# Stick-breaking attention on one core: two sliver tiles joined into one of 64 columns, and a few steps of the heads put at other units

## The chip, the cores and the metric

The kernel runs on one core of a Trainium2 chip. The metric is the device time of one execution in microseconds; the time before is 2059.08 us, the median of 3 runs (2058.46 to 2063.94). Engines are named as in the profile: PE (matmuls), PEld (its weight loads), DVE (vector), ACT (scalar), POOL (GpSimd) and SP (it issues the DMAs here).

## The reference, cut to what matters

One inference step of a decoder layer: a combined input projection, eight heads of stick-breaking attention and four of gated linear attention, a gate per branch, an output projection and two norms. There are 1024 prompt tokens behind 16 learned meta tokens (1040 rows) and 8 x 4 sampled tokens with paged caches. The change concerns the prompt's attention:

```python
def stick_break_weights(z, mask):
    sp = jnp.where(mask, jax.nn.softplus(z), 0.0)
    later = lax.cumsum(sp, axis=z.ndim - 1, reverse=True) - sp
    return jnp.where(mask, jnp.exp(jax.nn.log_sigmoid(z) - later), 0.0)

def sb_attend(qb, qpos, k, v, kpos, bias):
    a = stick_break_weights(sb_logits(qb, k, bias), kpos[None, :] < qpos[:, None])
    return jnp.einsum('bhqk,bkhd->bqhd', a.astype(v.dtype), v)
```

The mask is strict: a key counts only for later queries. The weight of a key is reduced by the softplus of all later keys that the query sees, so the work on one query goes from the last key to the first and hands a sum on (the carry).

## The kernel before, in words

Products of full float32 precision are made of three matmuls on a high part (rounded to float32r) and a low part (the rest): high by high, high by low, low by high. ACT makes a high part by a copy that rounds, DVE the low part by a subtraction.

**Heads.** `head(h)` runs the input projections of V, K and Q for one head, each by `inproj`: 16 blocks of rows for three chunks of tokens, in 24 groups of six matmuls into three PSUM accumulators (L342 to L344). After each group `W.beat()` moves a small scheduler, the Weaver, by one unit: whatever generator is due emits its next instructions there, up to its next `yield n`, which puts it off by n units. A head is 72 units. The attention of head h is woven in this way into the projections of head h+1. The order on each engine is then the program's order as the framework's scheduler sets it out; each engine works in its order, and waits on semaphores. A manual dependency without a semaphore (`spread`, `behind`) only sets that order: `spread` puts an instruction behind `W.mark`, the newest matmul of a projection.

**Tiles of attention.** Keys lie in nine tiles of 126 (`KT`) in the columns 1 to 126 of 128; column 0 holds the carry and column 127 nothing. Queries lie in two blocks, qi = 0 (positions 16 to 527) and qi = 1 (528 to 1039). `attend` spawns a tile per key tile and query block, from the last key tile to the first: (1,8) to (1,0), then (0,4) to (0,0). A tile has as many columns as queries that see some key of it. (1,8) has 32 and (0,4) has 24: these are the slivers. All others have 150 to 512.

`attend_tile` is one tile's generator:
- the scores z: three matmuls (L589 to L591) into a PSUM tile; X = softplus of z by DVE (L595, L598) and ACT (L596, L597); POOL's mask where the tile crosses the diagonal (L601);
- two units later, and when the predecessor's carry is there: the carry's copy into row 0 of X (L607), and the split of X, `hi_s` on ACT and `lo_s` on DVE (L574, L575 in `split_tmp`, which all splits share);
- D1 = 4 units later the correction: two matmuls with a triangle of -1 (L610, L611), which add to z; then Y = exp(z) on ACT (L615), its mask on POOL (L617), and in the same unit the split of Y, `hi_a` and `lo_a`;
- D2 = 6 units later the values: three matmuls (L623 to L625) into the query block's accumulator `O`; behind the block's last tile ACT copies it out (L628) and SP stores it (L629).

Unit by unit after the end of a head's Q projection, the scores, split of X, correction and values stand at 2, 4, 8, 14 for (1,8); at 40, 42, 46, 52 for (0,4); at 49, 54, 58, 64 for (0,1); at 53, 58, 62, 68 for (0,0).

**Keys and values of a head.** `ev_k` copies a chunk of projected keys to a staging tile and spawns `split_k`, which fills the two key tiles `kt` (high and low, one buffer each, so they come free with the last score matmul of the previous head, that of (0,0)): eight pieces in all, an ACT copy (L693) and a DVE subtraction (L694) for each, all pieces of a chunk in one unit. `load_v` runs in the three units behind the Q projection: a POOL memset of a staging tile (L561), the loads of V rows by 126 (L562, L564), the high part on ACT (L566), the low part on DVE (L568).

Around this, DVE works through the dot products of the sampled queries with the paged keys (L464), and SP issues the pages' loads. Staging tiles come from one pool of seven.

Of the kernel before, what the change touches and what calls it, by code (L numbers as in the profile page):

```python
# [10 lines left out]
F32 = mybir.dt.float32  # L11
# [5 lines left out]
ALU = mybir.AluOpType  # L17
# [3 lines left out]
P = 128  # L21
# [6 lines left out]
NSMP = NB * NT  # L28
T = META + SEQ + NSMP
REAL = META + SEQ  # L30
# [10 lines left out]
KT = 126  # L41
# [43 lines left out]
def hybrid_step(ctx: ExitStack, tc: tile.TileContext, x_prompt, x_sample, cache_k, cache_v, state_gla,  # L85
# [3 lines left out]
    nc = tc.nc  # L89
    mm = nc.tensor.matmul  # L90
    vec, act, pool = nc.vector, nc.scalar, nc.gpsimd
# [17 lines left out]
    W = Weaver()  # L109

    def stage(nm, dt=F32):
        return stg.tile([P, 384], dt, tag="stg", name=nm)
# [39 lines left out]
    znd = dram.tile([NSMP, HEADS, NSMP], F32, name="znd")  # L152
# [37 lines left out]
    with tc.tile_pool(name="xp", bufs=2) as xp, tc.tile_pool(name="xps", bufs=5, space=PSUM) as xps:  # L190
# [336 lines left out]
    with tc.tile_pool(name="sp", bufs=1) as sp, tc.tile_pool(name="sps", bufs=1, space=PSUM) as sps:  # L527
# [26 lines left out]
        def load_v(h, V, behind):  # L554

            for c in range(3):
                st = stage(f"vr{h}_{c}")
                sv = st[:].rearrange("p (a d) -> p a d", d=P)
                nt = 3 if c < 2 else 2
                src = new_v_prompt[0, 0, :, h, :]  # L560
                pool.memset(st[:], 0.0)  # L561
                nc.sync.dma_start(sv[1:KT + 1, :nt], src[c * 378:c * 378 + nt * KT].rearrange("(a p) d -> p a d", p=KT))  # L562
                if c == 2:
                    nc.sync.dma_start(sv[1:33, 2, :], src[8 * KT:REAL])  # L564
                vs = slice(3 * c, 3 * c + 3)
                ins = act.copy(V[0][:, vs, :], sv)  # L566
# [8 lines left out]
            vec.tensor_tensor(b[:rows, :n], X, a[:rows, :n].bitcast(F32), ALU.subtract)  # L575
            return a, b

        def attend_tile(h, qi, qlo, qhi, j, jmax, q, kt, V, carry, O):
            nm = f"{h}_{qi}_{j}"
            k0 = j * KT  # L580
            nk = P
            c0 = max(qlo, k0)
            col = c0 - qlo
            n = qhi - c0
            qs = slice(c0 - META, c0 - META + n)
            ks = slice(j * P, j * P + nk)
            z = sps.tile([P, 512], F32, tag="z", bufs=4, name=f"z{nm}")
            zz = z[:nk, :n]
            mm(zz, kt[0][:, ks], q[0][:, qs], start=True, stop=False)  # L589
            mm(zz, kt[0][:, ks], q[1][:, qs], start=False, stop=False)  # L590
            mm(zz, kt[1][:, ks], q[0][:, qs], start=False, stop=True)  # L591
# [3 lines left out]
            vec.tensor_scalar(X, zz, bias, 30.0, ALU.add, ALU.min)  # L595
# [4 lines left out]
            if w > 0:  # L600
                pool.affine_select(X[:, :w], X[:, :w], [[1, w]], ALU.is_gt, 0.0, base=c0 - k0 + 1, channel_multiplier=-1)  # L601
            yield 2
            if j < jmax:
# [6 lines left out]
            mm(zz, ntri0[:nk, :nk], sh[:nk, :n], start=False, stop=False, skip_group_check=True)  # L610
            mm(zz, ntri0[:nk, :nk], sl[:nk, :n], start=False, stop=True, skip_group_check=True)  # L611
# [4 lines left out]
            if w > 0:  # L616
                pool.affine_select(Y[:, :w], Y[:, :w], [[1, w]], ALU.is_gt, 0.0, base=c0 - k0 + 1, channel_multiplier=-1)  # L617
# [7 lines left out]
            mm(o[:, col:], V[1][:nk, j, :], ah[:nk, :n], start=False, stop=(j == 0), skip_group_check=True)  # L625
            if j == 0:
                st = sp.tile([P, 512], F32, tag="X", bufs=3, name=f"ost{h}_{qi}")
                act.copy(st[:], o[:])  # L628
                nc.sync.dma_start(od[h][:, qlo - META:qhi - META], st[:])  # L629

        def attend(h, q, kt, V):

            carry, O = {}, {}
            for qi, j in ORDER:
                qlo, qhi = ((16, 528), (528, REAL))[qi]
                n = qhi - max(qlo, j * KT)
                W.spawn(attend_tile(h, qi, qlo, qhi, j, (qhi - 1) // KT, q, kt, V, carry, O))
# [10 lines left out]
        def sample_q(h, qsm, ks):  # L648

            ps = sps.tile([P, 512], F32, tag="z", bufs=4, name=f"qst{h}")  # L650
            nc.tensor.transpose(ps[:NSMP, 0:P], qsm[:], ident[:])
            qtok = stage(f"qtok{h}")[:NSMP, :P]
            act.copy(qtok, ps[:NSMP, 0:P])
            nc.sync.dma_start(qsd[:, h * P:(h + 1) * P], qtok)
            ps = sps.tile([P, 512], F32, tag="z", bufs=4, name=f"zn{h}")
            mm(ps[:NSMP, :NSMP], ks[:], qsm[:], start=True, stop=True)
            zns = sp.tile([NSMP, NSMP], F32, tag="zns", name=f"zns{h}")
            act.copy(zns[:], ps[:NSMP, :NSMP])
            nc.sync.dma_start(znd[:, h, :], zns[:])
            yield 4  # L660
            heads_ready.append(h)

        def head(h):
# [15 lines left out]
            kt = [sp.tile([P, KW], F32R, tag=f"k{i}", name=f"k{i}_{h}") for i in range(2)]  # L679
# [3 lines left out]
            ks = sp.tile([P, NSMP], F32, tag="ks", name=f"ks{h}")  # L683

            def split_k(raw, c, lo, hi):
                at, end = lo, min(hi, REAL)
                while at < end:
                    j, off = divmod(at, KT)
                    n = max(1, (end - at) // KT) if off == 0 else 1
                    w = min(KT - off, end - at)  # L690
                    d = [t[:, j * P:(j + n) * P].rearrange("p (a x) -> p a x", a=n)[:, :, off + 1:off + 1 + w] for t in kt]
                    r = raw[:, at - lo:at - lo + n * w].rearrange("p (a x) -> p a x", a=n)
                    act.copy(d[0], r)  # L693
                    vec.tensor_tensor(d[1], r, d[0].bitcast(F32), ALU.subtract)  # L694
# [3 lines left out]
                return  # L698
                yield
# [21 lines left out]
            V = values(h, copied[-1])  # L721
# [15 lines left out]
    with tc.tile_pool(name="gp", bufs=1) as gp, tc.tile_pool(name="gps", bufs=1, space=PSUM) as gps:  # L737
# [323 lines left out]
        for g in range(GH):  # L1061
            kt = gp.tile([P, T], F32, tag="k", name=f"gk{g}")
# [227 lines left out]
    with ExitStack() as out:  # L1290
# [349 lines left out]
        kept = []  # L1640
# [53 lines left out]
```

## Time and profile before

| | |
|---|---|
| time, median of 3 runs | 2059.08 us |
| the profiled execution | 2062.69 us |
| its span | 2061.0 us |
| granted TensorE clock | 0.998 |
| head phase with attention | 116 to 960 us of the span, about |

The span reaches from the first to the last instruction of the program that the profile holds; the execution's time is a little longer. Busy time is the union of an engine's instructions. A matmul's start is exact, while its end is modelled, and matmuls that follow each other overlap; what one of them costs is read from the distance of starts. "Idle before" a group is the time that its engine had nothing to do just ahead of it, with what ended it.

### The profile page before, as it was taken

To read this page: it belongs to the slowest core of one execution; us is meant where nothing else is said; L and a number is where in the kernel's file an instruction comes from. 1 tells how busy PE (TensorE), PEld (TensorE's weight loads), DVE (VectorE), ACT (ScalarE), POOL (GpSimd) and SP (SyncE) were. 2 spreads that over 40 slices of the span, in tenths; PEclk is the share of its full clock that TensorE was granted. 3 is DMA by queue.
4 is the path that set the end of the run, shared out by engine and by line. 5 is a ranking of instruction groups with operands and counts; after the bars stand their busy time and mean duration, and the time that the engine had idled before them with its cause. 6 is when DMAs were issued, how large, how long until landed. Compare 5 with 4: busy or idle time off the path is not lost.

```text
span 2061.0 us, 41982 instructions
## 1 busy us (share of the span) xinstructions
PE 2023.1 (98%) x12507; PEld 1864.4 (90%) x12507; DVE 1551.5 (75%) x6282; ACT 953.5 (46%) x2293; POOL 85.1 (4%) x304
## 2 busy tenths in 40 slices
PE   6999999999999999999999999999999999999998
PEld 5999999999999998999999999999888898788776
DVE  7368989888988989899898888978444347554566
ACT  7355555565655556433534335343433325432332
POOL 0012000101000000000000000000000000000000
PEclk9999999999999999999999999999999999999999
DMA  6344454645455452443433434335776666352475
GB/s 202 104 139 147 140 158 134 169 134 147 146 157 147 141 126 73 138 107 80 108 103 80 126 81 115 93 87 166 241 228 230 222 227 195 134 163 75 148 272 175
DMA packets 371821, 301.85 MB, mean 146 GB/s; under 512 B 42360, under 2 KB 312104, under 8 KB 371592
## 3 DMA queue, kind: packets, MB, share of 16 engines
q1 hardware_dynamic: 371288, 298.64, 48.5%
q8 instruction: 98, 1.61, 0.3%
q14 instruction: 131, 1.07, 0.2%
q10 hardware_dynamic: 304, 0.53, 0.1%
HBM read 241.75 MB, written 57.31 MB: 145 GB/s over the span
## 4 chain that ended last, share of the span: by engine, by line
PE 84%; DVE 7%; DMA 3%; ACT 3%; issue 2%; SPq 1%; POOL 0%; DVEq 0%; ACTq 0%; POOLq 0%
PE acc_g L342 5%; PE acc_g L343 5%; PE acc_g L344 5%; PE b L1595 4%; PE b L1597 4%; PE b L1596 4%; PE acc_gv L342 3%; PE acc_gv L343 3%; PE acc_gv L344 3%; PE acc_k L342 3%; PE acc_k L344 3%; PE acc_k L343 3%; PE acc_v L342 2%; PE acc_v L344 2%; PE acc_v L343 2%; PE acc_q L342 2%
## 5 line engine op out<-in xcount | busy, mean ns | idle before, releaser
L464 DVE SCALAR_TENSOR_TENSOR jk<-kp,qb 128x128 f32<-128x128 f32 x2048 | 592.9, 289 | 43.2 <-DMA qb<-qsd 1.5
L342 PE MATMUL acc_g<-hT,wh_g 128*128 128x368 f32 (+2 forms) x768 | 251.1, 327 | 0.5 <-DVE ga L389 0.5
L343 PE MATMUL acc_g<-hT,wh_g 128*128 128x368 f32 (+2 forms) x768 | 247.2, 322 | 0.0
L344 PE MATMUL acc_g<-hT,wl_g 128*128 128x368 f32 (+2 forms) x768 | 246.8, 321 | 0.0
L1595 PE MATMUL b<-ring,f 128*128 128x512 f32 x416 | 164.7, 396 | 4.7 <-DVE u L1465 2.1
L464 DVE DVE_READ_ACCUMULATOR jk<-kp,qb 128x1 f32 x2048 | 166.7, 81 | 0.0
L1596 PE MATMUL b<-ring,f 128*128 128x512 f32 x416 | 163.3, 392 | 0.2 <-DVE ring L1395 0.2
L1597 PE MATMUL b<-ring,f 128*128 128x512 f32 x416 | 162.5, 391 | 0.0
L342 PEld LDWEIGHTS acc_g<-hT,wh_g 128*128 128x128 f32 x768 | 144.3, 188 | 13.1 <-issue 11.2
L1395 DVE TENSOR_TENSOR ring<-wr,ring 128x512 fp32r<-128x512 f32 x104 | 71.3, 689 | 102.4 <-ACT ring L1394 100.2
L343 PEld LDWEIGHTS acc_g<-hT,wh_g 128*128 128x128 f32 x768 | 144.4, 188 | 0.7
L344 PEld LDWEIGHTS acc_g<-hT,wl_g 128*128 128x128 f32 x768 | 144.2, 188 | 0.0
L1394 ACT CAST ring<-wr 128x512 fp32r<-128x512 f32 x104 | 64.2, 620 | 143.4 <-PE b L1597 83.7
L342 PE MATMUL acc_gv<-hT,wh_gv 128*128 128x400 f32 (+2 forms) x384 | 130.3, 339 | 0.0
L342 PE MATMUL acc_k<-hT,wh_k 128*128 128x384 f32 (+1 forms) x384 | 126.3, 329 | 0.0
L343 PE MATMUL acc_gv<-hT,wh_gv 128*128 128x400 f32 (+2 forms) x384 | 125.2, 326 | 0.0
L342 PE MATMUL acc_q<-hT,wh_q 128*128 128x368 f32 (+2 forms) x384 | 124.9, 325 | 0.0
L344 PE MATMUL acc_gv<-hT,wl_gv 128*128 128x400 f32 (+2 forms) x384 | 124.6, 325 | 0.0
L344 PE MATMUL acc_k<-hT,wl_k 128*128 128x384 f32 (+1 forms) x384 | 124.6, 324 | 0.0
L343 PE MATMUL acc_k<-hT,wh_k 128*128 128x384 f32 (+1 forms) x384 | 124.4, 324 | 0.0
L344 PE MATMUL acc_q<-hT,wl_q 128*128 128x368 f32 (+2 forms) x384 | 123.3, 321 | 0.0
L343 PE MATMUL acc_q<-hT,wh_q 128*128 128x368 f32 (+2 forms) x384 | 123.2, 321 | 0.0
(454 smaller groups left out, 5288.7 us busy)
## 6 DMA issues: line engine op xcount, KB each, us to landing
kp<-in_cache_k_dram SPq DMA_DIRECT2D x512, 64.0 KB
vr<-in_cache_v_dram SPq DMA_DIRECT2D x64, 512.0 KB
tf<-in_w_out_dram SPq DMA_DIRECT2D x64, 256.0 KB
td<-tf SPq DMA_DIRECT2D x64, 256.0 KB
qb<-qsd SPq DMA_DIRECT2D x64, 256.0 KB
wr_g<-in_w_in_dram SPq DMA_DIRECT2D x64, 256.0 KB
wr<-td SPq DMA_DIRECT2D x56, 256.0 KB
wr<-in_w_out_dram SPq DMA_DIRECT2D x48, 256.0 KB
```

The costliest lines, as they stand in the source:

```text
L342: mm(acc[c][:, :n], wh, hh[k][:, lo:hi], start=(k == 0), stop=False)
L343: mm(acc[c][:, :n], wh, hl[k][:, lo:hi], start=False, stop=False)
L344: W.mark = mm(acc[c][:, :n], wl, hh[k][:, lo:hi], start=False, stop=(k == NK - 1)).ins
L464: ins = vec.scalar_tensor_tensor(jk[:], kp[:], 1.0, qbs[h, b][:, t, :], ALU.mult, ALU.mult, accum_out=zt[:, t, NPG - 1 - i:NPG - i])
L1394: act.copy(wh, r)
L1395: vec.tensor_tensor(wl, r, wh.bitcast(F32), ALU.subtract)
L1595: mm(bk[:], ah, wh, start=first and k == 0, stop=False, skip_group_check=True)
L1596: mm(bk[:], ah, wl, start=False, stop=False, skip_group_check=True)
L1597: mm(bk[:], al, wh, start=False, stop=last and k == 7, skip_group_check=True)
```

## The change

- (1,8) and (0,4) run as one tile, j = 8, of 64 columns, first in the head: columns 0 to 31 are the last 32 queries of block 0, columns 32 to 63 the last 32 of block 1. Key tile 8 gets the 24 keys of (0,4) in its columns 32 to 55 (two POOL copies out of key tile 4), and V's rows for them come by one more load. Two POOL steps mask it (`causal`). The carry of block 0 is kept in a small SBUF tile, that of block 1 stays in PSUM. Its values go to an accumulator of their own, are copied to a small tile, and are added by DVE to the last 32 columns of each block's output behind the copy L628.
- (0,4) is no longer spawned, so (0,3) comes at unit 40. By the same counting the units of (0,1) are 47, 50, 54, 60 and those of (0,0) are 51, 54, 58, 64.
- In every tile the split of Y comes one unit behind Y (`yield 1`, then `D2 - 1`): the values stay where they were.
- `split_k` yields behind each piece, and chunk c begins 3c units later.
- The memsets of V's staging tiles are put behind `W.mark` by `spread`.
- The scores among sampled tokens (`zns`) take a staging tile in place of a tile of their own.

```diff
                 src = new_v_prompt[0, 0, :, h, :]
-                pool.memset(st[:], 0.0)
+                spread(pool.memset(st[:], 0.0))
...
                 if c == 2:
-                    nc.sync.dma_start(sv[1:33, 2, :], src[8 * KT:REAL])
+                    nc.sync.dma_start(sv[1:32, 2, :], src[8 * KT:REAL - 1])
+                    nc.sync.dma_start(sv[32:56, 2, :], src[4 * KT:4 * KT + 24])
...
+            both = j == 8
-            n = qhi - c0
+            n = 64 if both else qhi - c0
...
+            def queries(t):
+                if both:
+                    return t[:].rearrange("p (a x) -> p a x", a=2)[:, :, 480:512]
+                return t[:, qs]
+
+            def causal(t):
+                if both:
+                    t = t.rearrange("p (a x) -> p a x", a=2)
+                    pool.affine_select(t, t, [[1 - 24, 2], [1, 32]], ALU.is_gt, 0.0, base=24, channel_multiplier=-1)
+                    pool.memset(t[0:32, 0, :], 0.0)
+                elif w > 0:
+                    pool.affine_select(t[:, :w], t[:, :w], [[1, w]], ALU.is_gt, 0.0, base=c0 - k0 + 1,
+                                       channel_multiplier=-1)
...
-            carry[qi] = (j, zz, col)
+            if both:
+                kept = sp.tile([P, NSMP], F32, tag="ks", name=f"cy{h}")
+                act.copy(kept[0:1, :], z[0:1, 0:32])
+                carry[0], carry[1] = (4, kept, 480), (8, z[:, 32:64], 480)
+            else:
+                carry[qi] = (j, zz, col)
...
             act.activation(Y, zz, AF.Exp, bias=bias)
+            causal(Y)
+            yield 1
             ah, al = split_tmp(Y, nk, n, "a" + nm)
-            yield D2
+            yield D2 - 1
             if j == jmax:
                 O[qi] = sps.tile([P, 512], F32, tag="O", name=f"O{h}_{qi}")
+            if both:
+                o = sps.tile([P, 512], F32, tag="O", name=f"Ob{h}")[:, :n]
+                mm(o, V[0][:, j, :], ah[:, :n], start=True, stop=False, skip_group_check=True)
+                mm(o, V[0][:, j, :], al[:, :n], start=False, stop=False, skip_group_check=True)
+                mm(o, V[1][:, j, :], ah[:, :n], start=False, stop=True, skip_group_check=True)
+                O[2] = sp.tile([P, 64], F32, tag="ob", name=f"ob{h}")
+                act.copy(O[2][:], o)
+                return
...
                 act.copy(st[:], o[:])
+                vec.tensor_tensor(st[:, 480:512], st[:, 480:512], O[2][:, 32 * qi:32 * qi + 32], ALU.add)
...
-        ORDER = [(1, j) for j in range(8, -1, -1)] + [(0, j) for j in range(4, -1, -1)]
+        ORDER = [(1, j) for j in range(8, -1, -1)] + [(0, j) for j in range(3, -1, -1)]
...
-            zns = sp.tile([NSMP, NSMP], F32, tag="zns", name=f"zns{h}")
+            zns = stage(f"zns{h}")[:NSMP, :NSMP]
...
                     at += n * w
+                    yield 1
                 if c == 2:
+                    for t in kt:
+                        pool.tensor_copy(t[:, 8 * P + 32:8 * P + 56], t[:, 4 * P + 1:4 * P + 25].bitcast(F32))
                     act.copy(ks[:], raw[:, REAL - lo:hi - lo])
...
-                W.spawn(split_k(raw, c, lo, hi))
+                W.spawn(split_k(raw, c, lo, hi), 3 * c)
```

More of the change, by code (lines that the diff above doesn't have):

```diff
@@ L576, in split_tmp, with attend_tile @@
             return a, b
-        def attend_tile(h, qi, qlo, qhi, j, jmax, q, kt, V, carry, O):
+        def attend_tile(h, qi, qlo, qhi, j, q, kt, V, carry, O):
             nm = f"{h}_{qi}_{j}"
@@ L581, in attend_tile @@
             nk = P
+            both = j == 8
             c0 = max(qlo, k0)
             col = c0 - qlo
-            n = qhi - c0
+            n = 64 if both else qhi - c0
             qs = slice(c0 - META, c0 - META + n)
             ks = slice(j * P, j * P + nk)
+            def queries(t):
[10 more added lines that the diff above has]
+                                       channel_multiplier=-1)
             z = sps.tile([P, 512], F32, tag="z", bufs=4, name=f"z{nm}")
             zz = z[:nk, :n]
-            mm(zz, kt[0][:, ks], q[0][:, qs], start=True, stop=False)
-            mm(zz, kt[0][:, ks], q[1][:, qs], start=False, stop=False)
-            mm(zz, kt[1][:, ks], q[0][:, qs], start=False, stop=True)
+            mm(zz, kt[0][:, ks], queries(q[0]), start=True, stop=False)
+            mm(zz, kt[0][:, ks], queries(q[1]), start=False, stop=False)
+            mm(zz, kt[1][:, ks], queries(q[0]), start=False, stop=True)
             bias = bias0[:nk, h:h + 1]
@@ L599, in attend_tile @@
             w = min(n, k0 + KT - c0)
-            if w > 0:
-                pool.affine_select(X[:, :w], X[:, :w], [[1, w]], ALU.is_gt, 0.0, base=c0 - k0 + 1, channel_multiplier=-1)
+            causal(X)
             yield 2
-            if j < jmax:
+            jmax = (3, 7)[qi]
+            if not both:
                 while carry.get(qi, (None,))[0] != j + 1:
@@ L636, in attend @@
                 n = qhi - max(qlo, j * KT)
-                W.spawn(attend_tile(h, qi, qlo, qhi, j, (qhi - 1) // KT, q, kt, V, carry, O))
+                W.spawn(attend_tile(h, qi, qlo, qhi, j, q, kt, V, carry, O))
                 yield 2 if n < 100 else 3 if n < 200 else 4 if n < 450 else 5
         D1, D2 = 4, 6
-        ORDER = [(1, j) for j in range(8, -1, -1)] + [(0, j) for j in range(4, -1, -1)]
+        ORDER = [(1, j) for j in range(8, -1, -1)] + [(0, j) for j in range(3, -1, -1)]
         def values(h, behind):
@@ L656, in sample_q @@
             mm(ps[:NSMP, :NSMP], ks[:], qsm[:], start=True, stop=True)
-            zns = sp.tile([NSMP, NSMP], F32, tag="zns", name=f"zns{h}")
-            act.copy(zns[:], ps[:NSMP, :NSMP])
-            nc.sync.dma_start(znd[:, h, :], zns[:])
+            zns = stage(f"zns{h}")[:NSMP, :NSMP]
+            act.copy(zns, ps[:NSMP, :NSMP])
+            nc.sync.dma_start(znd[:, h, :], zns)
             yield 4
@@ L695, in split_k @@
                     at += n * w
+                    yield 1
                 if c == 2:
+                    for t in kt:
+                        pool.tensor_copy(t[:, 8 * P + 32:8 * P + 56], t[:, 4 * P + 1:4 * P + 25].bitcast(F32))
                     act.copy(ks[:], raw[:, REAL - lo:hi - lo])
-                return
-                yield
             def ev_k(c, ps, lo, hi):
```

2 lines of the change are left out of this document (removed).

## The prediction, made before the result was known

> **What bounds the kernel now.** First the page: the first line of its busy times, then the chain that ended last.
>
> ```profile
> PE 2023.1 (98%) x12507; PEld 1864.4 (90%) x12507; DVE 1551.5 (75%) x6282; ACT 953.5 (46%) x2293; POOL 85.1 (4%) x304
> ...
> PE 84%; DVE 7%; DMA 3%; ACT 3%; issue 2%; SPq 1%; POOL 0%; DVEq 0%; ACTq 0%; POOLq 0%
> ```
>
> TensorE is busy nearly always and carries most of the chain. All edits lie in the eight heads, so next comes the window view from the first score matmul of head 0 to well past the last head (columns: length, then busy time and count per engine, clock, DMA share, GB/s).
>
> ```profile
> core 0: us, PE busy (x) PEld busy (x) DVE busy (x) ACT busy (x) POOL busy (x), PEclk, DMA share, GB/s
> 116.00:960.00 844.00, 839.08 (x5161) 807.08 (x5160) 753.95 (x3482) 461.31 (x1104) 72.61 (x249) 1.00 0.48 135
> ```
>
> PE 839 of 844 us, at full clock; DVE 754, so 90 us to spare; ACT has 383. Time can go here in two ways only: fewer matmuls, or fewer waits of PE. The waits of PE in the same window:
>
> ```profile
> PE z L611 <- DVE lo_s L575: 2.7, 10, 0.8
> PE z L610 <- ACT hi_s L574: 1.2, 2, 0.9
> PE acc_v L342 <- ACT qsm L718: 0.4, 2, 0.2
> ```
>
> Nearly all idle time hangs on the two correction matmuls (L610, L611), which wait for the split of X (hi_s on ACT, lo_s on DVE). Matmul ends are modelled, so these sums understate a stall; start times say more.
>
> **Part 1: two sliver tiles become one.** Per head, (1,8) has 32 columns and (0,4) has 24: eight matmuls each (three scores, two corrections, three values). One tile with eight matmuls of 64 columns replaces them, so 64 matmuls go in eight heads. What is one worth? The score trio and the correction pair of a 24-column tile in the timeline of PE (start, length):
>
> ```profile
> 260.55 0.17 PE L589 MATMUL z<-q,k 128*128 128x24 f32 x1
> 260.58 0.26 PE L590 MATMUL z<-q,k 128*128 128x24 f32 x1
> 260.69 0.26 PE L591 MATMUL z<-q,k 128*128 128x24 f32 x1
> 260.80 0.42 PE L342 MATMUL acc_k<-hT,wh_k 128*128 128x384 f32 x1
> 261.06 0.34 PE L343 MATMUL acc_k<-hT,wh_k 128*128 128x384 f32 x1
> ```
>
> ```profile
> 268.56 0.17 PE L610 MATMUL z<-hi_s,ntri 128*128 128x24 f32 x1
> 268.59 0.26 PE L611 MATMUL z<-lo_s,ntri 128*128 128x24 f32 x1
> 268.70 0.42 PE L342 MATMUL acc_k<-hT,wh_k 128*128 128x384 f32 x1
> 268.97 0.33 PE L343 MATMUL acc_k<-hT,wh_k 128*128 128x384 f32 x1
> ```
>
> Lengths overlap, so only starts count. From the first sliver matmul to the second main one after it the trio takes 261.06 - 260.55 = 0.51 us. A main matmul of 384 columns alone keeps 0.17 us (in proportion to the 276 columns in 0.12 of the rows below), so the trio costs 0.34 and the pair 0.41 - 0.17 = 0.24. The value trio has the trio's shape: 0.34. A tile is 0.92 us, about 0.115 a matmul; eight tiles are **7.4 us**.
>
> ```profile
> 267.15 0.29 PE L589 MATMUL z<-q,k 128*128 128x276 f32 x1
> 267.27 0.29 PE L590 MATMUL z<-q,k 128*128 128x276 f32 x1
> ```
>
> The kept tile of 64 columns lies between 24 columns (0.11 a matmul) and 276 (0.12): at most 0.01 more each, 0.7 us over 64 matmuls. I count 0.3. The strided query operand has no row; nothing to the same 0.7 covers it.
>
> [...]
>
> Off PE a sliver takes with it four DVE operations and five of ACT a head, and adds two of DVE (the sliver columns' sums behind L628), two of ACT (the kept carry, the copy of the sliver output) and two POOL copies of keys. A small DVE operation, and the copy of O behind which the new sums come:
>
> ```profile
> L595 DVE TENSOR_SCALAR X<-z,bias 128x24 f32<-128x24 f32 x8 | 1.9, 237 | 0.0
> L628 ACT COPY ost<-O 128x512 f32<-128x512 f32 x16 | 9.4, 588 | 16.0 <-PE O L625 15.8 <-DVE lo_a L575 0.2
> ```
>
> At 0.24 us apiece DVE has some 0.5 us less a head, and ACT three operations less. Neither is the bound (90 and 383 us to spare): nothing. What it costs without that cover is the second rival. POOL masks a tile in two steps now, but one tile less, so four steps a head as before; its key copies wait for the last key piece (unit 57), with the mask of (0,0)'s Y (unit 58) queued behind them, 0.3 us each by the mask's row below. That goes into the 0.5 us at the end.
>
> **Part 2: the split of Y moves one unit back, V's memsets are tied, key pieces are spread.** These act on the stall. The same place in head 2, PE first, then POOL, ACT and DVE:
>
> ```profile
> 284.16 0.32 PE L344 MATMUL acc_q<-hT,wl_q 128*128 128x368 f32 x1
> 284.54 0.45 PE L610 MATMUL z<-hi_s,ntri 128*128 128x402 f32 x1
> 285.15 0.45 PE L611 MATMUL z<-lo_s,ntri 128*128 128x402 f32 x1 [0.16 <-DVE lo_s L575]
> 285.44 0.33 PE L342 MATMUL acc_q<-hT,wh_q 128*128 128x384 f32 x1
> ```
>
> ```profile
> 282.58 0.78 POOL L561 MEMSET vr<- 128x384 f32 x2 [3.02 <-ACT st_k L546]
> 283.31 0.29 POOL L617 TENSOR_SCALAR_AFFINE_SELECT Y<-Y 128x126 f32<-128x126 f32 x1
> ...
> 283.64 0.42 ACT L574 CAST hi_a<-Y 128x276 fp32r<-128x276 f32 x1 [0.59 <-POOL Y L617]
> 283.97 0.52 ACT L574 CAST hi_s<-X 128x402 fp32r<-128x402 f32 x1
> ...
> 284.09 0.45 DVE L575 TENSOR_TENSOR lo_a<-Y,hi_a 128x276 fp32r<-128x276 f32 x1 [0.34 <-ACT hi_a L574]
> 284.52 0.58 DVE L575 TENSOR_TENSOR lo_s<-X,hi_s 128x402 fp32r<-128x402 f32 x1
> ```
>
> Read backwards: PE waits for lo_s, which stands behind lo_a on DVE and hi_s on ACT; hi_s stands behind hi_a; hi_a waited 0.59 us for POOL's mask of Y, which stood behind two memsets of V's staging, whose loads are issued from 289.11 on (below). From 284.16 to 285.44 PE spends 1.28 us, where 0.17 and twice 0.18 (402 columns at the rate of 276 in 0.12) would do: 0.75 lost. Is it so in every head? The groups by form:
>
> ```profile
> L611 PE MATMUL z<-lo_s,ntri 128*128 128x402 f32 x8 | 3.6, 450 | 2.2 <-DVE lo_s L575 2.1
> L610 PE MATMUL z<-hi_s,ntri 128*128 128x402 f32 x8 | 3.1, 385 | 1.0 <-ACT hi_s L574 0.9
> ```
>
> All eight of the 402-column tile have a long mean, with 3.2 us idle ahead of them. The stall lies between 3.2 (idle alone) and 6.0 us (0.75 x 8). In the new order hi_s and lo_s of the next tile come one unit ahead of hi_a and lo_a of this one, so the critical pair gains what hi_a and lo_a took ahead of it: 0.33 on ACT and 0.43 on DVE, and the 0.59 of waiting for the mask: more than the 0.6 us that L610 and L611 were late. The memsets leave POOL's queue there as well. (0,1), freed of a predecessor tile, splits X at unit 50 instead of 54, before the key tiles come free at 51 (score matmul of (0,0), 53 before), so the eight key pieces no longer crowd it. I take 4.5 us, nearer the timeline. The other waits on these lines and on qsm (4.3 in the first view less 3.0 in these rows, 1.3) may give 0.9.
>
> What is late next is the split of Y: it now has five units until its value matmuls instead of six. A unit's length:
>
> ```profile
> L566 ACT CAST V<-vr x24: 501/512/517, 114.9 to 766.1; 128x384 fp32r<-128x384 f32 x24
> ```
>
> First to last V cast is seven heads, 651 us or 93 a head of 72 units: 1.3 us a unit. Five units are 6.5 us against the 0.42 and 0.45 of hi_a and lo_a in the rows: covered.
>
> The tied memsets move V's loads from here
>
> ```profile
> 289.11 1.36 SPq L562 DMA_DIRECT2D vr<-out_dram  x3
> ...
> 293.60 0.35 SPq L564 DMA_DIRECT2D vr<-out_dram  x1
> ```
>
> to units 1 to 3 after the head's end (301 us: the first cast, 114.9, marks that of head 0, two heads earlier), with one SP issue more a head (0.35). Its key-8 part is needed by the first value matmul at unit 14: eleven units, 14 us, for a memset, four issues, a landing, a cast of 0.51 and a subtraction. ACT's queue waits at the cast, with the first tiles' exponentials behind it. Counted at nothing to 8 x 0.1; I take 0.5 us for these and the rest of new waits.
>
> **Sum.** -7.4 + 0.3 - 4.5 - 0.9 + 0.5 = **-12 us**. The profiled execution took 2062.69 us (span 2061.0), so 2050.7 there; the median shown is 3.6 lower, and **2059.08 - 12 = 2047 us** is the forecast. About 0.3%, 6.2 us, is what a measurement of this kernel can tell from no change: the line lies at 2052.9.
>
> **Rivals.**
> - *The stall stays.* The key tiles come free two units earlier, so the key pieces still crowd ACT and DVE, now beside (0,0). For it: the correction waits sit where the pieces are. Against: hi_a and the memsets stand directly ahead of hi_s in the rows. Then only 7.4 - 0.3 - 0.5 = 6.6: 2052.5.
> - *New waits on ACT and DVE.* L628 waited 15.8 us in all for O, and the new sums on DVE now queue behind it, lo_s behind them; the sliver output's copy waits likewise on ACT. At 1 us of wait 16 times that is 16 of DVE's 90 spare us. If a third of it reached PE, 5 us come back: 2052.
> - *V late, slower than before.* If SP's queue of key pages holds the tied V loads until past unit 14, PE stands in every head at the merged tile's value matmuls. It decides once the loads land 14 us after the head's end; each us beyond costs 8. It is slower than no change from 1.5 us beyond, by 0.3% from 2.3; at 2.5: 2059 - 12 + 20 = 2067. Against: the loads were issued 7 us ahead of the casts before, without PE ever waiting for V.
> - *The slivers were nearly free* (the merge does not shorten PE): only the 0.03 us interval goes, 64 x 0.03 = 1.9, and the sum is -1.9 + 0.3 - 5.4 + 0.5 = -6.5: 2052.6. [...] Against: the 0.11 us steps.
>
> **How the numbers follow.** Forecast 0.64 (2043 to 2051); stall stays 0.14; new waits 0.10; V late 0.08; slivers free 0.04. The middle three straddle 2052.9: I give half of stall and slivers to faster (0.09), the rest with the new waits (0.19) to the same. Faster 0.73, same 0.19, slower 0.08. The range runs from 2042 (both terms at their upper ends, 7.4 + 6.0 + 1.3, and 2 us of scatter) to 2057, above the middle cases, leaving V late out.
>
> **What would show it.** Right: PE instructions fall by about 64 (plus as many weight loads); intervals of the 64-column rows stay near 0.11 us; L610 and L611 of 402 columns show no idle; memsets of vr start after the query phase. Wrong: a new releaser of PE, such as V or O; a DVE wait on the copy of O of several us just ahead of lo_s; or busy time of PE down by much more or less than 7 us in 116 to 960.

## The result, and the profile after

The changed kernel takes 2062.89 us (median of 12 runs, 2061.0 to 2066.2); the kernel before, beside it on the chip, 2059.43 (12 runs). The ratio is 1.0019, 95% interval 1.0011 to 1.0027: slower by 0.2%, some 4 us, where 12 us less was forecast. The profiled execution of the changed kernel took 2062.32 us (span 2060.6), that of before 2062.69; single executions scatter more than this difference, so the profiles show where time went, and the sizes are taken from the ratios.

TensorE's busy line of the page after, and the window view of the heads (length, busy time and count of PE, PEld, DVE, ACT and POOL, clock, DMA share, GB/s):

```profile
PE 2017.2 (98%) x12443; PEld 1858.8 (90%) x12443; DVE 1550.2 (75%) x6266; ACT 949.6 (46%) x2269; POOL 93.0 (5%) x320
```

```profile
116.00:960.00 844.00, 833.46 (x5086) 801.25 (x5085) 751.59 (x3456) 456.68 (x1081) 79.43 (x263) 1.00 0.48 136
```

Exactly 64 matmuls and 64 weight loads are gone, as foreseen. But in the same stretch PE is busy 5.6 us less than before, and it has done 75 matmuls less: the eleven that are missing beside the 64 say that it has fallen behind. The matmuls were removed, and idle time stands in their place. Its waits in this stretch, and the groups of correction matmuls by shape (busy, mean ns, idle ahead of them and its releaser):

```profile
PE z L627 <- DVE lo_s L576: 5.0, 10, 2.0
PE z L626 <- ACT hi_s L575: 3.1, 6, 0.7
PE acc_g L342 <- DVE ga L389: 1.6, 1, 1.6
```

```profile
L627 PE MATMUL z<-lo_s,ntri 128*128 128x512 f32 x48 | 19.2, 400 | 2.1 <-DVE lo_s L576 2.0
L627 PE MATMUL z<-lo_s,ntri 128*128 128x410 f32 x8 | 3.4, 421 | 1.0 <-DVE lo_s L576 1.0
L626 PE MATMUL z<-hi_s,ntri 128*128 128x410 f32 x8 | 3.3, 415 | 2.4 <-ACT hi_s L575 2.4
L627 PE MATMUL z<-lo_s,ntri 128*128 128x402 f32 x8 | 2.8, 349 | 0.0
```

The idle time ahead of the 402-column tile (0,1), at the end of a head, is gone. It stands now ahead of the 410-column tile (1,5) near the start of a head, and ahead of one 512-column tile. Two new things thus have to be found: what is late at a head's start, and what holds the one big tile. These rows of the waits of ACT and DVE in the same stretch, first of before, then of after, show what has grown there (ACT's wait for `acc_q`, ahead of its copies of Q, has grown too, from 12.5 to 27.5 us):

```profile
ACT ost L628 <- PE O L625: 15.8, 7, 2.3
...
ACT V L566 <- DMA vr<-out_dram: 2.2, 3, 1.8
...
DVE V L568 <- ACT V L566: 1.7, 1, 1.7
```

```profile
ACT ost L657 <- PE O L654: 31.8, 7, 5.6
...
ACT V L567 <- DMA vr<-out_dram: 18.7, 13, 4.4
...
DVE V L569 <- ACT V L567: 13.3, 12, 4.1
...
DVE ost L658 <- ACT ost L657: 8.9, 6, 3.0
```

ACT waited 13 times for V's loads, 18.7 us in all, where it had been 3 times and 2.2 us, and DVE waited behind it. Here is one such place, the end of head 5's projections: GpSimd's memsets of the staging tiles, then SP's issues, ACT and DVE (start, length, idle before):

```profile
567.67 1.13 POOL L561 MEMSET vr<- 128x384 f32 x3
```

```profile
582.95 0.40 SPq L562 DMA_DIRECT2D vr<-out_dram  x1
...
584.59 1.37 SPq L421 DMA_DIRECT2D kp<-in_cache_k_dram  x1
...
586.82 0.31 SPq L565 DMA_DIRECT2D vr<-out_dram  x1
587.02 0.51 ACT L567 CAST V<-vr 128x384 fp32r<-128x384 f32 x1 [2.20 <-DMA vr<-out_dram]
...
587.57 0.56 DVE L569 TENSOR_TENSOR V<-vr,V 128x384 fp32r<-128x384 f32 x1 [2.05 <-ACT V L567]
...
589.67 0.22 DVE L576 TENSOR_TENSOR lo_s<-X,hi_s 128x64 fp32r<-128x64 f32 x1
```

The same place before:

```profile
579.07 0.42 SPq L564 DMA_DIRECT2D vr<-out_dram  x1
580.54 0.92 ACT L566 CAST V<-vr 128x384 fp32r<-128x384 f32 x2
...
586.46 0.19 DVE L575 TENSOR_TENSOR lo_s<-X,hi_s 128x32 fp32r<-128x32 f32 x1
```

Before, the last load was issued 1.5 us ahead of the first cast, and the first tile's split stood at 586.46. After, five loads come from 582.95 to 586.82, with a page of keys between them that takes 1.37 us to issue, and the first cast can only start at 587.02; the first tile's hi_s is queued behind it on ACT (587.44), and its lo_s is at 589.67. Some 1.4 of these 3.2 us were there already: ACT's copy of the last 272 columns of Q starts at 580.25 before and at 581.65 after. In all eight heads of the changed kernel the last of V's loads is issued 3.9 to 6.5 us behind the last matmul of the projection of Q; before, this was so in one head, by 2.4 us. The tie carries no semaphore, and GpSimd ran ahead of it all the same: the memsets were done at 568.8, 14 us before the first load. What moved is the place of the loads in SP's order: the store `zd` (L469) is issued behind all of them before, at 582.11, and ahead of all of them after, at 582.52. What ACT and DVE still have to do for the head's first tiles is queued behind those casts. In head 4 such a load is on the chain of waits itself (start, length):

```profile
482.46 7.28 DMA wr_v<-in_w_in_dram
...
489.81 6.01 DMA vr<-out_dram
...
495.84 0.52 ACT V L567
```

Among the five longest pieces of the chain there is none of V before.

### The profile page after: what moved, and what is told of

It is laid out like the page before. It is cut to its first block, busy times and chain, and to the rows that moved or that the text cites. A ratio compares the mean times of both kernels' runs of the same rounds, so it can differ in the third digit from the quotient of the medians.

```text
span 2060.6 us, 41822 instructions
## 1 busy us (share of the span) xinstructions
PE 2017.2 (98%) x12443; PEld 1858.8 (90%) x12443; DVE 1550.2 (75%) x6266; ACT 949.6 (46%) x2269; POOL 93.0 (5%) x320
## 4 chain that ended last, share of the span: by engine, by line
PE 83%; DVE 7%; DMA 4%; ACT 3%; issue 2%; POOL 0%; SPq 0%; DVEq 0%; ACTq 0%; POOLq 0%
PE acc_g L342 6%; PE acc_g L343 6%; PE acc_g L344 6%; PE b L1626 4%; PE b L1627 4%; PE b L1628 4%; PE acc_gv L342 3%; PE acc_gv L343 3%; PE acc_gv L344 3%; PE acc_k L342 3%; PE acc_k L344 3%; PE acc_k L343 3%; PE acc_q L342 3%; PE acc_q L343 3%; PE acc_q L344 2%; DVE jk L464 2%
```

## The experiments

The first theory: the tie of the memsets moves V's loads behind the head's end, and this costs more than the rest gains. Rivals: the merged tile itself gives its matmuls back through the sums behind the copy of O; the later split of Y or the spread key pieces do harm. Each ratio is to the kernel before, run beside the other; its 95% interval is in brackets.

**The changed kernel without the tie.**

```diff
-                spread(pool.memset(st[:], 0.0))
+                pool.memset(st[:], 0.0)
```

> The changed kernel with the memsets of V's staging not tied (one word of the change undone). Theory V (the tie puts V's loads behind the end of the head; ACT waits 18.7 us for their landing, DVE 13.3 us behind ACT, and the next splits of X come late to PE): ACT's wait for the landing falls back under 4 us, PE's waits in 116 to 960 us fall by some 8 us, the ratio to before is about 0.996 (2051 us). Rival O (the merged tile's own new waits, the sums behind the copy of O and the copy of the sliver output, eat the gain): the ratio stays near 1.002. Rival Y (the split of Y, put one unit later, crowds the next tile): it stays near 1.002 as well.

Measured: 2059.18 us, 0.9994 [0.9985, 1.0003], no different from before. The tie costs some 0.25% in the changed kernel, but without it the change is still far from its forecast, and ACT still waits 8.0 us for V's loads, at 6 places, where under 4 us were expected.

**One part at a time, added to the kernel before:** the tie; the merged tile (with the move of `zns` and of the load of its keys); the later split of Y; the spread key pieces.

```diff
-                pool.memset(st[:], 0.0)
+                spread(pool.memset(st[:], 0.0))
```

> The kernel before with the tie of the memsets alone. Theory V: slower by 5 to 12 us, ratio 1.003 to 1.006, ACT waiting for V's landing by 10 to 20 us in all. Rivals O and Y: no difference from before, 0.999 to 1.001, or faster by the POOL queue that the memsets leave (the forecast counted on that, some 2 us).

Measured: 2067.24, 1.0036 [1.0023, 1.0049]. ACT's wait for the loads is there again without any merged tile:

```profile
ACT V L566 <- DMA vr<-out_dram: 18.8, 13, 3.1
```

```diff
+            both = j == 8
-            n = qhi - c0
+            n = 64 if both else qhi - c0
...
-        ORDER = [(1, j) for j in range(8, -1, -1)] + [(0, j) for j in range(4, -1, -1)]
+        ORDER = [(1, j) for j in range(8, -1, -1)] + [(0, j) for j in range(3, -1, -1)]
```

> The merged tile alone: no tie, the split of Y in its old unit, key pieces as before. Theory V: the 7 us of 64 matmuls come, ratio 0.996 to 0.998, and the stall at the 402-column tile stays or shrinks. Rival O: ratio 1.000 or above, with DVE's wait for the copy of O of 9 us or more ahead of late splits of X.

Measured: 2065.41, 1.0024 [1.0015, 1.0034]. With 64 matmuls less it is *slower* than before.

```diff
             act.activation(Y, zz, AF.Exp, bias=bias)
...
+            yield 1
             ah, al = split_tmp(Y, nk, n, "a" + nm)
-            yield D2
+            yield D2 - 1
```

> The kernel before with the split of Y one unit later alone. The forecast's step (the next split of X gets ahead of this split of Y): the stall at L610 and L611 of the 402-column tile goes from about 6 us to under 2, ratio 0.997 to 0.999. Rival Y: ratio 1.001 or above.

Measured: 2054.35, 0.9969 [0.9957, 0.9981]. This is all that PE waits for in the stretch of the heads:

```profile
PE acc_g L342 <- DVE ga L389: 0.7, 1, 0.7
PE z L611 <- DVE lo_s L575: 0.2, 1, 0.2
```

```diff
                     at += n * w
+                    yield 1
...
-                W.spawn(split_k(raw, c, lo, hi))
+                W.spawn(split_k(raw, c, lo, hi), 3 * c)
```

> The kernel before with the key pieces spread alone (one piece a unit, chunk c 3c units later). The forecast gave it a share of the stall at the 402-column tile. Theory: the pieces are few and short, ratio 0.998 to 1.000. Rival: with the staging tiles held longer something else waits, ratio above 1.001.

Measured: 2059.57, 0.9994 [0.9984, 1.0004]: nothing.

**The changed kernel with V's memsets and loads 16 units into Q's projection,** casts where they were. The tie stays.

```diff
+        def fetch_v(h, got):
...
+                yield 1
+
+        def load_v(h, V, behind, got):
...
+            W.spawn(fetch_v(h, got), 16)
```

> The changed kernel, memsets still tied, but memset and loads of V spawned 16 units into the Q projection (8 units before its end), with the casts where they were. Theory V (it is the late landing that costs, not the tie): ACT's wait for the landing under 3 us, at least as fast as the untied kernel (0.9994), about 0.996 to 0.999. Rival: the memset's place in POOL's queue costs, then as slow as the changed kernel, 1.002.

Measured: 2053.69, 0.9966 [0.9955, 0.9976]; ACT no longer waits for V at all. Against the changed kernel's 1.0019 the late loads cost 0.5%, some 11 us. It is their lateness and not the tie: the tie is still there.

**The sums behind the copy of O on GpSimd,** so that DVE doesn't wait for that copy; on the merged tile alone, and with the later split of Y.

```diff
-                vec.tensor_tensor(st[:, 480:512], st[:, 480:512], O[2][:, 32 * qi:32 * qi + 32], ALU.add)
+                pool.tensor_tensor(st[:, 480:512], st[:, 480:512], O[2][:, 32 * qi:32 * qi + 32], ALU.add)
```

> The merged tile alone, with the two sums of the sliver columns done by POOL in place of DVE. Theory O (the sums wait on DVE for the copy of O, 10 us in all, and the dot products and the splits and evacuations of Q behind them run late into the next head): DVE's wait for the copy goes to 0, PE's waits fall by 4 to 8 us, ratio 0.997 to 0.999 against 1.0024 with the sums on DVE. Rival (the merged tile is late for other reasons: two POOL steps in its chain, the copies of carry and sliver output): ratio stays at 1.001 or above.

> The same with the split of Y one unit later; no tie, key pieces as before. If the parts add up: 7 us of the merge and 6.4 of the split of Y, 2046 to 2049 us, ratio 0.993 to 0.995, and PE's waits in 116 to 960 us under 2 us. Rival as for the run with POOL sums: 0.997 or above.

Measured: 2066.58, 1.0029 [1.0018, 1.0039], and with the split 2064.1, 1.0015 [1.0005, 1.0026]. The wait has moved from DVE to GpSimd, and nothing is gained:

```profile
POOL ost L657 <- ACT ost L656: 58.3, 15, 7.5
```

So DVE's wait for the copy of O is not the price of the merge by itself. How much of it is, this test can't say: the wait was moved to another in-order queue, V's loads are still late in both kernels (ACT waits 8.8 and 10.7 us for them), and the second is slower than the changed kernel without the tie (1.0015 against 0.9994), which has its sums on DVE and differs besides only in the key pieces.

**Is it late V again?** In the run with the merged tile alone ACT waits for V too, though nothing is tied:

```profile
ACT V L567 <- DMA vr<-out_dram: 6.7, 4, 2.4
```

Four kernels: early loads (the edit of `fetch_v` above) with the merged tile, alone, and with the merged tile and the later split of Y; and the kernel before with its last row of V fetched by a load of its own:

```diff
-                    nc.sync.dma_start(sv[1:33, 2, :], src[8 * KT:REAL])
+                    nc.sync.dma_start(sv[1:32, 2, :], src[8 * KT:REAL - 1])
+                    nc.sync.dma_start(sv[32:33, 2, :], src[REAL - 1:REAL])
```

> The merged tile alone with V's memsets and loads spawned 8 units before the end of the Q projection, untied. The traces of the merge alone show V's loads issued up to 5 us behind the head's end in four heads (one of eight before), and ACT's casts waiting for them. Theory V2 (the merge is slow because its loads of V come late, as with the tie): all loads are issued before the head's end, ACT waits under 3 us for V, the ratio falls from 1.0024 to 0.997 to 0.999. Rival (the merge's own chain, carry and sliver copies, is what costs): 1.001 or above, with the loads early.

> The kernel before with the same early memsets and loads of V alone. Theory V2: the loads were early in seven of eight heads already, so little is to be had: 0.998 to 1.000. Rival (early loads are a gain of their own, whatever the rest): 0.997 or below.

> Merge, the split of Y one unit later, and early loads of V; key pieces as before, no tie. If the two steps that the forecast counted on add up once V is on time: 0.993 to 0.995 (2047 to 2050 us). If the merge costs what it saves even so: 0.997, as the split of Y alone.

> The kernel before with one more load of V a head (the last row of key tile 8 by a load of its own), nothing else. Theory V2 in its simplest form (one more issue in SP's queue puts the loads past the head's end): ratio 1.001 to 1.004, loads late in more heads than one. Rival (the order of the queue with the merged tile, not the count, does it): 0.999 to 1.001.

| kernel | us | ratio to before |
|---|---|---|
| merged, early V | 2059.39 | 0.9990 [0.9982, 0.9999] |
| early V alone | 2058.32 | 0.9991 [0.9982, 0.9999] |
| merged, split of Y later, early V | 2056.1 | 0.9972 [0.9961, 0.9983] |
| one load more, alone | 2061.32 | 1.0004 [0.9996, 1.0013] |

Early loads mend the merged tile from 1.0024 to 0.9990, so late V was part of its price (an additional load alone is none). But then it is worth no more than early loads alone, and with the later split no more than that split alone (0.9969). Seven microseconds of matmuls still bring nothing. In the third of these kernels PE's longest wait, 2.2 us, is at a single place, the 512-column tile (0,0) of head 0. The timeline of PE, of GpSimd and of DVE there, then the windows of one microsecond:

```profile
190.56 0.32 PE L344 MATMUL acc_q<-hT,wl_q 128*128 128x368 f32 x1
191.20 0.50 PE L632 MATMUL z<-hi_s,ntri 128*128 128x512 f32 x1 [0.32 <-ACT hi_s L581]
193.92 0.50 PE L633 MATMUL z<-lo_s,ntri 128*128 128x512 f32 x1 [2.22 <-DVE lo_s L582]
```

```profile
189.21 0.67 POOL L607 TENSOR_SCALAR_AFFINE_SELECT X<-X 128x110 f32<-128x110 f32 x1 [2.38 <-DVE X L620]
189.83 0.88 POOL L401 TENSOR_SCALAR_AFFINE_SELECT lv<-lv 128x64 f32<-128x64 f32 x2
...
191.03 0.83 POOL L403 TENSOR_SCALAR_AFFINE_SELECT lv<-lv 128x64 f32<-128x64 f32 x2
```

```profile
191.89 0.66 DVE L406 CAST lvl<-lv 128x128 uint8<-128x128 f32 x1 [1.87 <-POOL lv L403]
...
193.17 0.69 DVE L582 TENSOR_TENSOR lo_s<-X,hi_s 128x512 fp32r<-128x512 f32 x1
```

```profile
194.00:195.00 1.00, 1.00 (x5) 0.95 (x6) 0.93 (x6) 0.54 (x1) 0.00 (x0) 0.81 0.49 160
195.00:196.00 1.00, 1.00 (x5) 1.00 (x4) 0.90 (x6) 0.62 (x2) 0.72 (x3) 0.50 0.55 184
196.00:197.00 1.00, 1.00 (x6) 1.00 (x5) 0.96 (x5) 0.14 (x1) 1.00 (x2) 0.50 0.16 45
197.00:198.00 1.00, 1.00 (x5) 1.00 (x4) 0.49 (x3) 0.62 (x1) 0.14 (x1) 0.50 0.35 89
198.00:199.00 1.00, 1.00 (x7) 1.00 (x7) 0.94 (x4) 0.00 (x0) 0.00 (x0) 0.99 0.19 48
```

GpSimd builds masks for a later stage here (`level_masks`, lines 399 to 403: one level every 16 units, seven in all), and DVE casts each (L406). With the merged tile the scores of (0,0) come two units earlier, and so GpSimd's mask of X of (0,0) at 189.21, which itself waited 2.38 us for DVE, now stands *ahead* of the level mask's steps. DVE's cast waits 1.87 us for them, the split of X stands behind the cast, and PE starts a single matmul between 190.56 and 193.92. Then it runs at half the clock (0.50 in the rows) until about 198: matmuls of 384 columns start 0.32 us apart from 194.91 on, where it was 0.18 from 194.25 to 194.61. In the kernel before, the steps of this level mask (the last at 189.36) come ahead of the mask of X, and the cast at 190.22 has no wait (GpSimd, then DVE):

```profile
189.36 0.83 POOL L403 TENSOR_SCALAR_AFFINE_SELECT lv<-lv 128x64 f32<-128x64 f32 x2
...
190.76 0.27 POOL L601 TENSOR_SCALAR_AFFINE_SELECT X<-X 128x110 f32<-128x110 f32 x1
```

```profile
190.22 0.42 DVE L406 CAST lvl<-lv 128x128 uint8<-128x128 f32 x1
```

The same collision stands in all eight kernels that have the merged tile and DVE's cast: DVE waits 1.8 to 1.9 us at this cast, and one matmul of PE 2.0 to 2.3 us behind it. Seven of them show a granted clock of 0.77 to 0.83 over the ten microseconds from 190; six kernels without the merged tile have 1.00.

So the new theory: a single collision, worth the stall of 2.2 and 0.3 us and, by estimate, half of some 3.4 us at half clock (0.4 us of the microsecond from 194, three whole ones after it), 4 us together. The test is to let GpSimd cast the mask that it has built, so that DVE never waits for it, with a control: the same kernel without the merged tile, with and without this edit; and the edit in the whole changed kernel with early V.

```diff
-            vec.tensor_copy(lvl[m][:], a)
+            pool.tensor_copy(lvl[m][:], a)
```

> The merged tile, the split of Y one unit later and the early loads of V (as in the run before), and VectorE no longer casts the level masks: GpSimd casts the mask that it has just built. In the run without this edit VectorE waited 1.9 us at the cast in head 0, right ahead of the split of X of the 512-column tile, the products of that tile waited 2.2 us for it, and TensorE was busy 7.46 of the 10 us from 190 with a granted clock of 0.83 there. Theory (the 7 us of the merge are given back in a few places where an in-order queue stands behind something that the merge has shifted, and this is the largest): about 3 us less, 2053 us, ratio 0.9957; the wait at the cast is gone, TensorE is busy over 9.7 us of the ten and the clock is 1.00. Rival 1 (the merge gives back its time everywhere, because VectorE and ScalarE set the pace): unchanged within 1 us, 2056, the wait moves to another instruction. [...]

> Before's kernel, with two sliver tiles, with the split of Y one unit later and V's loads early: the same as the kernel of merged tile, later split and early loads, but for the merge, so that the difference of the two is the merge alone with all loads on time. Theory (the merge gives back all of its 7 us): 2052.5 to 2055, ratio 0.996 to 0.9975, that is the same as with the merge. Rival (the merge is worth its 7 us once V is on time): 2061 to 2063, no better than before, which the split of Y alone at 0.9969 speaks against.

> The run with two sliver tiles, later split of Y and early loads, with the level masks cast by GpSimd: the control of that edit. VectorE waited only 0.6 us for level masks before, so both theories give the same time as without it, within 0.8 us. If it gains 2 us or more, the edit has another effect than to take away the wait in head 0, and what it gains with the merge can't be put down to that wait.

> The changed kernel whole, with V's memsets and loads 16 units into the projection of Q (measured 0.9966 so), and the level masks cast by GpSimd. Theory: VectorE's 1.8 us wait in head 0 goes with its stall, about 3 us less, 2050.5 us, ratio 0.995, the best of all. Rival (pace set elsewhere): 2053.5, ratio 0.9966 as without the edit.

| kernel | us | ratio to before |
|---|---|---|
| merged, split later, early V, mask cast by GpSimd | 2052.26 | 0.9958 [0.9944, 0.9971] |
| not merged, split later, early V | 2054.96 | 0.9974 [0.9963, 0.9984] |
| the same, mask cast by GpSimd | 2054.45 | 0.9973 [0.9962, 0.9984] |
| the changed kernel, early V, mask cast by GpSimd | 2051.41 | 0.9956 [0.9942, 0.9970] |

With the merged tile the edit takes 0.9972 to 0.9958, 2.9 us by the ratios and 3.8 by the medians; their intervals overlap, so the traces have to carry the verdict. These are the ten microseconds from 190 with DVE's cast (first row) and with GpSimd's (second row), each from its own kernel:

```profile
190.00:200.00 10.00, 7.46 (x34) 6.81 (x33) 7.15 (x38) 3.22 (x6) 4.34 (x11) 0.83 0.36 106
```

```profile
190.00:200.00 10.00, 9.52 (x55) 8.73 (x54) 8.15 (x43) 3.58 (x8) 4.99 (x13) 1.00 0.43 120
```

55 matmuls start there in place of 34, at full clock (1.00); PE is busy 9.52 us of the ten, a little less than the 9.7 expected. In the control the edit does nothing (0.9974 and 0.9973), so it works through the collision that comes with the merged tile. The changed kernel itself shows the same dip, 0.83 with 39 matmuls.

The lengths of the heads in the traces say it more sharply than the times. Each is taken from the start of the first matmul of one head's projection of V to that of the next, in us, and named by the head whose attention is woven into it:

| kernel (one execution each) | head 0 | 1 | 2 | 3 | 4 | 5 |
|---|---|---|---|---|---|---|
| merged, split later, early V | 96.2 | 92.4 | 90.9 | 91.0 | 91.1 | 91.5 |
| the same, mask cast by GpSimd | 92.4 | 92.6 | 90.9 | 91.0 | 91.1 | 91.4 |
| not merged, split later, early V | 92.2 | 91.7 | 92.0 | 92.1 | 91.7 | 92.2 |
| the same, mask cast by GpSimd | 92.4 | 91.7 | 92.0 | 92.1 | 91.7 | 91.9 |

The edit takes 3.8 us from head 0 of the merged kernel, and changes no other head, nor any head of the control, by more than some 0.2. So the collision is shown, and its size with it. In the changed kernel with early V the same edit takes head 0 from 95.5 to 91.8; its time alone (0.9956, with 0.9966 inside its interval) could not have told the theory from the rival.

And the merged tile is at last worth something: 0.9958 against 0.9973 of its control, 3 us (2.2 by the medians) of its seven; these intervals overlap too. The table shows where it pays, with 1.1 us less in heads 2 and 3 and 0.5 to 0.6 in heads 4 and 5, and where it doesn't: nothing in head 0, and 0.9 more in head 1. The rest stands in smaller waits of the edited kernel:

```profile
PE z L633 <- DVE lo_s L582: 1.7, 4, 1.1
PE acc_v L342 <- ACT qsm L756: 1.5, 1, 1.5
PE acc_g L342 <- DVE ga L389: 1.0, 1, 1.0
PE z L632 <- ACT hi_s L581: 0.3, 1, 0.3
```

4.5 us in all, against 1.1 (0.7 at `ga`, 0.4 at lo_s) in its control. That these are the missing four was not tried by taking them away; it is what the rows suggest. The longest of them is late V once more: in head 1, at 211.09 us, PE waits 1.50 us for `qsm`, which on ACT stands behind two casts of V that have waited 0.81 and 0.63 us for their loads. The changed kernel with early V and GpSimd's cast, 0.44% faster than before, has the lowest time of all that ran; the merged tile with the later split and the same two edits is at no measurable distance from it.

## Why the prediction was wrong, by its steps

**What bounds the kernel** was right: PE, whose time goes by matmuls or by waits.

**The merged tile, -7.4 and +0.3.** The count is right, and so is the price of the tile that stays: from the first start of its correction pair to the next main matmul go 0.13 us, where the pair of 24 columns took 0.14 (268.56 to 268.70 in the prediction). Over all heads, reckoned from starts as the prediction does, a median pair costs 0.227 us with 24 columns and 0.223 with 64, a score trio 0.337 and 0.338, a value trio 0.333 and 0.338. So 0.9 us a head or 7.2 us of matmuls went, and the 0.3 for the wider tile was not needed.

```profile
590.51 0.19 PE L626 MATMUL z<-hi_s,ntri 128*128 128x64 f32 x1
...
590.64 0.39 PE L342 MATMUL acc_v<-hT,wh_v 128*128 128x304 f32 x1
```

Why the second matmul of a score trio starts only 0.03 us behind the first (260.55 and 260.58 in the prediction's rows) is not shown: PEld has a load for each of the three, recorded 0.02 to 0.03 us ahead of the second (260.56) and of the third (260.66) alike, and the third starts 0.11 us behind the second. In the kernel the first two have the same weights, the high part of the keys.

The step that failed is the one behind it: "Neither is the bound (90 and 383 us to spare): nothing." Spare time over the whole stretch says nothing of where an instruction stands in a queue. The merge moved (0,3) to (0,0) earlier against all else in the program, a masking step of GpSimd went ahead of another, and 4 us went at one tile of one head. Alone, the merged tile cost 0.24%, and part of that was late V: 0.9990 with early loads.

**The stall of the 402-column tile, -4.5, and other waits, -0.9.** Right: the later split of Y alone gives 0.31%, 6.4 us, where 5.4 were forecast, and leaves PE hardly a wait. Of the reasons given, one sufficed: hi_s and lo_s come ahead of hi_a and lo_a. That the memsets would leave GpSimd's queue, counted as help, did not come about as a gain in any run (the tie alone loses), and the key pieces at other units change nothing.

**V's loads behind the head's end, "counted at nothing to 8 x 0.1; I take 0.5 us".** This is the step that turned the sign. The late loads cost some 11 us in the changed kernel (1.0019 against 0.9966), and the tie that makes them late costs 0.36% alone. The text had even said that "ACT's queue waits at the cast, with the first tiles' exponentials behind it", and then compared the landing only with the first value matmul, 14 us on. The rival *V late* had the cause right and the point from which it decides wrong: PE needs no V for 14 us and more (in head 5 of the changed kernel the first value matmul starts at 598.08, 17 us behind the last matmul of Q's projection at 580.92), but ACT and DVE stop at the casts one to three units behind the head's end, and the splits of X that PE needs stand behind them. The reading against it, that "the loads were issued 7 us ahead of the casts", holds for head 2, where it was taken; over the eight heads of the kernel before, the last load is issued from 13.5 us ahead of the first cast (head 0) to 1.4 us behind it (head 4), so three heads had hardly any room to lose.

**The rival *new waits on ACT and DVE***, through the sums behind the copy of O, saw waits that came (DVE 8.9 us, ACT's wait for O up from 15.8 to 31.8). Moving DVE's to GpSimd gained nothing, and ACT's was not taken away in any run (27.7 us are left in the kernel with GpSimd's cast), so what they cost stays open. *The stall stays* is refuted by the 402-column row, which has no idle time ahead of it now, *slivers free* by the intervals above and by the heads that are 1.1 us shorter with the merged tile.

Put together, from 12 us less to 4 us more there are 16 to explain. Late V is 11 of them. The collision at the level mask is 2 by this kernel's pair of ratios (0.9966 and 0.9956), 3 by the other pair, 4 by the trace. With both away the change is worth 0.44%, 9 us; up to 3 us are left, for which the rows suggest small waits that were not taken away one by one. The traces, one execution each, agree on the two causes and size them differently. From the first matmul of head 1's projection of V to the first of `acc_ga`, behind the last head's projections, the kernel before takes 650.4 us, the changed kernel 650.8, with early V 643.2, with GpSimd's cast as well 639.3: 7.6 for late V, 4.0 for the collision, and 11 of the forecast 12 us in hand once both are gone.

## What to carry to other kernels

Here a wait on an in-order queue was paid by what stood behind it there, not by the consumer of what was waited for: ACT waited 18.7 us for V's loads and DVE 13.3 us behind it, and the late loads cost some 11 us, though in head 5 the first value matmul starts only at 598.08, 11 us behind the first cast of V. So for each wait that an edit adds, look at the next instruction of that engine on which the bounding engine depends, and take the time until that one as the slack. Where an edit shortens a chain that is woven into others, everything behind it changes its place in all queues, so list the neighbours of the moved instructions on each engine (those of foreign tasks above all) before counting the saving. And when several edits come together, measure them one by one: here one gain of 0.3% and a saving of matmuls lay hidden under two bad steps.

## What the runs showed of the hardware that was not expected

One stall cost PE more than its length. In the run with the collision (merged, split later, early V) PE waited 0.32 and 2.22 us at the 512-column tile (0,0) of head 0 and started one matmul between 190.56 and 193.92, and head 0 took 96.2 us; with the mask cast by GpSimd it waited 0.26 and 0.23 us there, and head 0 took 92.4: 3.8 us for some 2 us more of waits. The granted clock was 0.81, 0.50, 0.50 and 0.50 in the four microseconds from 194 and back at 0.99 in the fifth; some 3.4 us at half rate are, by estimate from these rows, another 1.7 us lost. In the kernel without this stall the same ten microseconds from 190 have 1.00. But the stall's length does not settle it: the merged kernel with its sums on GpSimd and the later split has a wait of 2.2 us for lo_s too, and PE is busy 7.49 us of these ten as against 7.46, yet their granted clock is 1.00. What decides between the two is not shown.
